# A decoder layer's FFNs: up products as seven products of half size in each dimension, tokens in quarters of 258

## The chip, the cores and the metric

The kernel runs on one core of a Trainium2 chip. The metric is the device time of one execution in microseconds. Five engines work side by side, each in the order of its own instructions, and wait for one another by semaphores: PE (TensorE, matrix products into PSUM), DVE (VectorE), ACT (ScalarE), POOL (GpSimd) and SP (SyncE, which issues most of the transfers).

## What is computed

One layer of a decoder for 1024 prompt tokens and 8 sample tokens, 1032 in all, with a width D of 1024: an FFN, a token mix (windowed attention and a gated branch), another FFN, and a last norm. All is float32. The part that the change touches is the FFN, which runs twice:

```python
def swiglu(h, w_up, w_down):
    a, b = jnp.split(h @ w_up, 2, axis=-1)
    return (jax.nn.silu(a) * b) @ w_down

def pre(i, t):
    return rms_norm(t, norm_g[i]) * (1 + mod[:, :, 3 * i + 1]) + mod[:, :, 3 * i]

x = x + 0.5 * mod[:, :, 2] * swiglu(pre(0, x), ffn1_up, ffn1_down)
```

`w_up` is 1024 x 5632 (two halves of D_FF = 2816, one for a and one for b), `w_down` 2816 x 1024. The shifts, scales and gates `mod` come from a product of the condition with `ada_w` (adaLN).

## The kernel before

**Layout.** Rows of weights lie on the 128 partitions, tokens along the free dimension. A large product gives 128 output rows for one chunk of tokens. The chunks `CH` are 384, 384 and 264 tokens wide. Both factors are split into a high and a low float32r part, and each product runs in three passes: high by high, high by low, low by high. `mm_chunk` (line 298) does this: it takes a PSUM buffer from the pool `ps_mm`, which has three, and for each k of the contraction issues the three matmuls of lines 306, 307 and 308.

**The FFN.** `ffn` (line 611) goes through 22 tiles of hidden rows in groups of `PARTS` (4, 4, 4, 4, 4, 2). For a tile and a chunk `up_a` makes the a half: ACT's tanh reads the PSUM buffer (line 626), DVE multiplies it with the same buffer (line 628). `up_b` makes the b half: DVE multiplies (line 641), ACT and DVE split the result into high and low part (642, 644). When a group is complete, its part of the down product is added to x in SBUF (`down_job`, `gated_add`, line 603, with lines 607 and 608 for the sample tokens). So up and down products alternate through the FFN.

**The weights** come as a stream of slabs of up to 1 MB, issued by SP (`fill_loads`, line 233); ACT copies the high part (272), DVE subtracts for the low part (273). Side work (adaLN products, norms, copies of caches) is cut into steps, and `tick()` between the matmuls advances it.

**The norm** (`norm`, line 539) reads x and writes high and low part of its result to tiles of their own: DVE multiplies (581), ACT adds the shift (583), DVE subtracts (571). The sums of squares are squared on ACT (486) and added on POOL (492).

**The start.** SP loads the adaLN weights of the first norm, the rows of x, the first slabs of `ffn1_up`; x is transposed by PE, and `mm_two` (line 318, matmuls 325 to 327) begins the first tile. x stays in SBUF through the first FFN and is copied to DRAM (`xs_d`) when each chunk of it is done.

## Time and profile before

| | us |
|---|---|
| median of 3 runs | 2422.71 (2422.45 to 2422.93) |
| span of the profiled execution | 2421.1 |
| PE busy | 2388.4 (99%) |
| PE weight loads busy | 2296.7 |
| DVE busy | 972.6 (40%) |
| ACT busy | 591.9 (24%) |
| POOL busy | 191.9 (8%) |

All later sums are made against the span; the median of the runs is 1.6 us longer, what lies around the program. Busy time of PE overlaps, since matmuls are pipelined: the distance of two starts tells the rate. PE's weight loads run beside its matmuls. An engine's idle time is listed with what released it, and idle time of an engine that isn't the bottleneck costs nothing.

### The profile page before, as it was taken

To read this page: it belongs to the slowest core of one execution; us is meant where nothing else is said; L and a number is where in the kernel's file an instruction comes from. 1 tells how busy PE (TensorE), PEld (TensorE's weight loads), DVE (VectorE), ACT (ScalarE), POOL (GpSimd) and SP (SyncE) were. 2 spreads that over 40 slices of the span, in tenths; PEclk is the share of its full clock that TensorE was granted. 3 is DMA by queue.
4 is the path that set the end of the run, shared out by engine and by line. 5 is a ranking of instruction groups with operands and counts; after the bars stand their busy time and mean duration, and the time that the engine had idled before them with its cause. 6 is when DMAs were issued, how large, how long until landed. Compare 5 with 4: busy or idle time off the path is not lost.

```text
span 2421.1 us, 36144 instructions
## 1 busy us (share of the span) xinstructions
PE 2388.4 (99%) x15567; PEld 2296.7 (95%) x15567; DVE 972.6 (40%) x1887; ACT 591.9 (24%) x1140; POOL 191.9 (8%) x285
## 2 busy tenths in 40 slices
...
GB/s 288 70 70 87 122 88 106 52 135 92 140 157 105 154 145 64 142 156 140 119 108 98 75 123 219 175 84 57 70 36 53 53 35 47 59 36 35 70 18 71
DMA packets 140649, 239.15 MB, mean 99 GB/s; under 512 B 6505, under 2 KB 98385, under 8 KB 139722
## 3 DMA queue, kind: packets, MB, share of 16 engines
...
q14 instruction: 37, 0.30, 0.0%
...
## 4 chain that ended last, share of the span: by engine, by line
PE 96%; DVE 1%; ACT 1%; DMA 1%; issue 0%; POOL 0%; DVEq 0%; SPq 0%; POOLq 0%; ACTq 0%
PE mm L306 30%; PE mm L307 29%; PE mm L308 29%; PE sc L398 1%; PE sc L986 1%; PE pv L1038 1%; DMA big<-in_ada_w_dram 1%; PE pt L1021 0%; PE mm L1021 0%; PE pt L421 0%; PE sc L1312 0%; DVE big L571 0%; PE ms L1237 0%; PE pt L1237 0%; DVE big L603 0%
## 5 line engine op out<-in xcount | busy, mean ns | idle before, releaser
L306 PE MATMUL mm<-big,hi 128*128 128x384 f32 (+1 forms) x4400 | 1420.0, 323 | 0.5 <-DVE t L1394 0.5
L308 PE MATMUL mm<-big,lo 128*128 128x384 f32 (+1 forms) x4400 | 1400.6, 318 | 0.0
L307 PE MATMUL mm<-big,hi 128*128 128x384 f32 (+1 forms) x4400 | 1400.0, 318 | 0.0
L306 PEld LDWEIGHTS mm<-big,hi 128*128 128x128 f32 x4400 | 827.0, 188 | 44.5 <-issue 26.1
L307 PEld LDWEIGHTS mm<-big,hi 128*128 128x128 f32 x4400 | 827.5, 188 | 0.2 <-DVE big L571 0.2
L308 PEld LDWEIGHTS mm<-big,lo 128*128 128x128 f32 x4400 | 826.2, 188 | 0.0
L272 ACT ACTIVATE hi<-raw 128x1024 fp32r<-128x1024 f32 (+1 forms) x186 | 194.1, 1043 | 448.3 <-PE mm L307 352.8
L273 DVE TENSOR_TENSOR lo<-raw,hi 128x1024 fp32r<-128x1024 f32 (+1 forms) x181 | 219.5, 1213 | 164.0 <-ACT hi L272 163.4
L603 DVE SCALAR_TENSOR_TENSOR big<-mm,MOD,big 128x384 f32<-128x384 f32 (+1 forms) x288 | 164.0, 571 | 235.9 <-PE mm L308 235.8
L628 DVE SCALAR_TENSOR_TENSOR t<-t,mm 128x384 f32<-128x384 f32 (+1 forms) x132 | 67.6, 512 | 287.7 <-ACT t L626 287.6
L641 DVE TENSOR_TENSOR t<-t,mm 128x384 f32<-128x384 f32 (+1 forms) x132 | 67.6, 512 | 276.4 <-PE mm L308 276.3
L642 ACT ACTIVATE big<-t 128x384 fp32r<-128x384 f32 (+1 forms) x132 | 64.9, 491 | 453.3 <-DVE t L641 453.3
L626 ACT ACTIVATE t<-mm 128x384 f32<-128x384 f32 (+1 forms) x132 | 60.4, 457 | 324.5 <-PE mm L308 324.5
L492 POOL TENSOR_TENSOR ph<-ph,t 128x384 f32<-128x384 f32 (+1 forms) x42 | 39.0, 930 | 797.4 <-ACT t L486 796.3
L644 DVE TENSOR_TENSOR big<-t,big 128x384 fp32r<-128x384 f32 (+1 forms) x128 | 66.2, 517 | 71.5 <-ACT big L642 71.5
L492 POOL TENSOR_TENSOR big<-big 128x384 f32<-128x384 f32 (+1 forms) x20 | 18.4, 921 | 721.8 <-ACT big L486 721.0
L1010 ACT ACTIVATE t<-t,s 128x128 f32<-128x128 f32 (+1 forms) x96 | 42.1, 439 | 80.3 <-DVE s L1005 72.8
L890 ACT ACTIVATE t<-mm 128x384 f32<-128x384 f32 (+1 forms) x48 | 21.9, 457 | 128.7 <-PE mm L308 92.8
L583 ACT ACTIVATE big<-t,MOD 128x384 fp32r<-128x384 f32 (+1 forms) x72 | 41.2, 579 | 47.8 <-DVE t L581 47.4
L571 DVE SCALAR_TENSOR_TENSOR big<-t,MOD,big 128x384 fp32r<-128x384 f32 (+1 forms) x72 | 46.6, 647 | 2.1 <-ACT big L583 2.1
L918 DVE COPY big<-mm 128x384 f32<-128x384 f32 x18 | 13.3, 741 | 59.7 <-PE mm L308 59.7
L306 PE MATMUL mm<-big 128*128 128x384 f32 (+1 forms) x96 | 33.0, 344 | 2.9 <-DVE big L603 2.2
...
## 6 DMA issues: line engine op xcount, KB each, us to landing
...
```

Source lines behind the costliest of these rows:

```text
L272: nc.scalar.activation(h3, v, AF.Copy)
L273: lo_eng[0].tensor_tensor(l3, v, h3.bitcast(FT), op=ALU.subtract)
L306: mm_f(ps[:, :n], wh, ah, start=(k == 0), stop=False)
L307: mm_f(ps[:, :n], wh, al, start=False, stop=False)
L308: mm_f(ps[:, :n], wl, ah, start=False, stop=(k == K - 1))
L492: nc.gpsimd.tensor_tensor(accs[c][0], accs[c][0], s, op=ALU.add)
L603: nc.vector.scalar_tensor_tensor(x[:, m, c0:e1], ps[:, :n], MOD[:, gate + m, 0:1], src[:, :n], op0=ALU.mult, op1=ALU.add)
L626: nc.scalar.activation(t[:, :w], pa[:, :w], AF.Tanh, scale=0.5)
L628: nc.vector.scalar_tensor_tensor(u[:, :w], t[:, :w], 1.0, pa[:, :w], op0=ALU.add, op1=ALU.mult)
L641: nc.vector.tensor_tensor(u[:, :w], u[:, :w], pb[:, :w], op=ALU.mult)
L642: nc.scalar.activation(g[:, s, c0:c1], u[:, :w], AF.Copy)
L644: eng.tensor_tensor(g[:, 4 + s, c0:c1], u[:, :w], g[:, s, c0:c1].bitcast(FT), op=ALU.subtract)
```

## The change

**Up products by Strassen's scheme.** The four blocks of a product of two by two blocks are a (two token quarters) and b (two token quarters): the contraction of 1024 is cut in two halves, the tokens of a pair in two quarters of 258 (256 of the prompt, 2 samples), and the output rows are the a and the b tile of one hidden tile. Instead of eight products of half the contraction there are seven, between sums and differences of the blocks. The sums over the tokens are made once in each FFN and pair of quarters (`pair_norm`, seven operands `H`), those of the weights for each hidden tile (`take`, on POOL). Products 0, 2, 4 and 6 are added up in the first of three accumulators of PSUM, product 1 goes to the second, 3 and 5 to the third (`ACC`); an accumulator has one bank for each of the two pairs. Results are read between the products (`finish`). One hidden tile for both pairs is a turn of 7 x 2 x 12 matmuls; the first two hidden tiles are done for pair 0 and then for pair 1, as four turns with one pair.

**Order.** All up products of an FFN come first, their gated results go to DRAM (`g_d`); the down products follow in `PARTS` (2, 4, 4, 4, 4, 4), with g loaded back and split, and x loaded back from `xs_d` or `x2_d`. All other large products run over four quarters of 258 tokens instead of three chunks.

**PSUM and SBUF.** The PSUM pools give way to one tile `PSB` whose eight banks are dealt out by stage. The norm works in place on x, and x is saved to DRAM ahead of it (`keep_x`).

The constants and the deal of the banks:

```diff
-PARTS = (4, 4, 4, 4, 4, 2)
-CH = ((0, 384), (384, 768), (768, 1032))
-ORD = (2, 0, 1)
+PARTS = (2, 4, 4, 4, 4, 4)
+QW = 258
+PW = 516
...
+    PSB = psp.tile([P, 8, 512], FT, name="PSB")
...
+    UPPER = dict(sc=(6,), pt=(7,), pv=(1,), ms=(3,))
+    LOWER = dict(two=(2, 4, 0), pt=(7,), pv=(6,), ms=(7,))
```

The large products outside of the up products:

```diff
-    def mm_chunk(w, j, K, act, c, k0=0):
...
+    def mm_chunk(w, j, K, act, c):
+
+        ps = bank("mm")[:, :QW]
...
-            if k % 2 == 1 and k < K - 1:
+            mm_f(ps, wh, ah, start=(k == 0), stop=False)
+            mm_f(ps, wh, al, start=False, stop=False)
+            mm_f(ps, wl, ah, start=False, stop=(k == K - 1))
+            if k in (2, 5) and k < K - 1:
```

The norm in place, the seven operands, and the copy of x:

```diff
+    def halves(t):
+
+        w = qb(FR, "h")
+        hi, lo = (four(w[:, z:z + 1032]) for z in (0, 1032))
+        nc.scalar.activation(hi, t, AF.Copy)
+        nc.vector.tensor_tensor(lo, t, hi.bitcast(FT), op=ALU.subtract)
+        return w
...
+    def pair_norm(i, p, rs, b0, blocks, stop=False, xs=None):
...
+            for k in range(4 * h, 4 * h + 4):
+                v = x[h][:, k % 4]
+                nc.vector.scalar_tensor_tensor(two(v), two(v), MOD[:, gp + k, 0:1], pb, op0=ALU.mult, op1=ALU.mult)
+                nc.scalar.activation(v, v, AF.Identity, bias=MOD[:, sh + k, 0:1])
...
+        H = OPS[p] = [None] * 7
+        f = nc.gpsimd.tensor_tensor
+        t3 = [tt().rearrange("p (k t) -> p k t", k=2) for _ in range(2)]
+        H[0] = halves(B[0][0])
+        for z in range(2):
+            f(t3[z], B[1][1][:, 2 * z:2 * z + 2], B[0][1][:, 2 * z:2 * z + 2], op=ALU.subtract)
+        f(B[0][1], B[0][1], B[0][0], op=ALU.subtract)
+        yield
+        H[1] = halves(B[1][0])
+        for z in range(2):
+            v = B[0][0][:, 2 * z:2 * z + 2]
+            f(v, v, t3[z], op=ALU.add)
+        yield
+        H[2] = halves(B[0][0])
+        yield
+        w = H[3] = qb(FR, "h")
+        for z in range(2):
+            hi, lo = (w[:, o_ + z * PW:o_ + z * PW + PW].rearrange("p (k t) -> p k t", k=2) for o_ in (0, 1032))
+            nc.scalar.activation(hi, t3[z], AF.Copy)
+            nc.vector.tensor_tensor(lo, t3[z], hi.bitcast(FT), op=ALU.subtract)
+        yield
+        nc.vector.tensor_tensor(B[1][0], B[1][0], B[0][0], op=ALU.subtract)
+        H[4] = halves(B[0][1])
+        yield
+        H[5] = halves(B[1][0])
+        yield
+        H[6] = halves(B[1][1])
...
+    def keep_x(p, dst):
+        for h in range(2):
+            nc.sync.dma_start(dst[:, 4 * h:4 * h + 4, p * PW:(p + 1) * PW], XT[p][h])
```

The up products, their weights, and what is read from PSUM when (`prepare` is the split of the weights before and `take` of these):

```diff
+    class Up:
+
+        ACC = (0, 1, 0, 2, 0, 2, 0)
+        AHEAD = 6
...
+            self.turns = [(0, (0,)), (1, (0,)), (0, (1,)), (1, (1,))] + [(n, (0, 1)) for n in range(2, NF)]
...
+        def take(self, s):
+            if s >= self.n:
+                return
+            n, j = divmod(s, 7)
+            a1, a2, b1, b2 = (self.raw[n][:, q * 512:(q + 1) * 512] for q in range(4))
+            w = hip.tile([P, 1024], FR, tag="hi", name=nm("hi")) if s % 2 else lop.tile([P, 1024], FR, tag="lo", name=nm("lo"))
+            f = nc.gpsimd.tensor_tensor
+            src = (a1, a2, a1, a1, b1, b2, a2)[j]
+            if j == 2:
+                f(b1, b1, b2, op=ALU.add)
+                f(a1, b1, a1, op=ALU.subtract)
+            elif j == 3:
+                f(a2, a2, a1, op=ALU.subtract)
+                f(a1, b2, a1, op=ALU.subtract)
+            self.wt[s] = w, src
...
+        def product(self, s):
+            n, j = divmod(s, 7)
+            w, _ = self.wt.pop(s)
+            go = dict(skip_group_check=True)
+            for p in self.turns[n][1]:
+                out = PSB[:, 2 * self.ACC[j] + p, :QW]
+                for kk in range(4):
+                    wh, wl = w[:, kk * 128:(kk + 1) * 128], w[:, 512 + kk * 128:512 + (kk + 1) * 128]
+                    h = OPS[p][j]
+                    ah, al = h[:, kk * QW:(kk + 1) * QW], h[:, 1032 + kk * QW:1032 + (kk + 1) * QW]
+                    mm_f(out, wh, ah, start=(kk == 0 and j in (0, 1, 3)), stop=False, **go)
+                    mm_f(out, wh, al, start=False, stop=False, **go)
+                    mm_f(out, wl, ah, start=False, stop=(kk == 3), **go)
+                    if kk % 2:
+                        tick()
...
+            def gate(v):
+                u = new()
+                nc.scalar.activation(u, v, AF.Tanh, scale=0.5)
+                nc.vector.scalar_tensor_tensor(u, u, 1.0, v, op0=ALU.add, op1=ALU.mult)
+                return u
+
+            if j == 0:
+                t["a"] = new()
+                nc.scalar.activation(t["a"], acc(0), AF.Copy)
+            elif j == 1:
+                nc.vector.tensor_tensor(t["a"], t["a"], acc(1), op=ALU.add)
+                t["u"] = gate(t.pop("a"))
+            elif j == 2:
+                t["b"] = new()
+                nc.scalar.activation(t["b"], acc(0), AF.Copy)
+            elif j == 3:
+                t["c"] = new()
+                nc.scalar.activation(t["c"], acc(2), AF.Copy)
+            elif j == 4:
+                nc.vector.tensor_tensor(t["c"], t["c"], acc(0), op=ALU.add)
+            elif j == 5:
+                nc.vector.tensor_tensor(t["b"], t["b"], acc(2), op=ALU.add)
+                u = t.pop("u")
+                nc.gpsimd.tensor_tensor(u, u, t.pop("b"), op=ALU.mult)
+                store(u, 0)
+            else:
+                u = gate(acc(0))
+                nc.gpsimd.tensor_tensor(u, u, t.pop("c"), op=ALU.mult)
+                store(u, 1)
+
+        def run(self, hook):
+            for s in range(self.n):
+                n, j = divmod(s, 7)
+                if j == 1:
+                    self.load(n + 2)
+                self.prepare(s + self.AHEAD)
+                if n < 4 and j == 0:
+                    require(self.turns[n][1][0])
+                self.product(s)
+                self.finish(s)
+                hook(n, j)
```

The down products (`split` makes high and low part of g on ACT and DVE, `job` is one down product with its gated addition):

```diff
+    class Down:
...
+        def load(self, i):
+            if i < len(PARTS):
+                self.raw[i] = self.rows([qb(name="g") for _ in range(self.count(i))], i)
+                for p in range(2):
+                    nc.gpsimd.dma_start(self.raw[i][p], self.src[:, self.FIRST[i]:self.FIRST[i] + PARTS[i],
+                                                                 p * PW:(p + 1) * PW])
...
+        def run(self, then, final):
+            dealing(**LOWER)
+            ahead = None
+            for i in range(len(PARTS)):
+                if ahead in hi_q:
+                    hi_q.remove(ahead)
+                    for _ in ahead:
+                        pass
+                if i == len(PARTS) - 1:
+                    run([self.job(i, m, p, qs, then) for p, qs in final for m in range(8)])
+                    return
+                ahead = self.split(i + 1, 6 if i == 0 else 0)
+                hi_q.append(ahead)
+                if i:
+                    self.load(i + 2)
+                run([self.job(i, m, p, (0, 1), lambda *_: None) for n in range(0, 8, 2) for p in range(2) for m in (n, n + 1)])
```

The order of the start:

```diff
+    for t in range(4):
         load_x(t)
-    fill_loads()
+    up1.load(0)
...
+    up1.load(1)
+    for t in range(4, 8):
         load_x(t)
+    nc.sync.dma_start(cst[:, C_M0:], a["consts"][:, C_M0:])
...
+    for t in range(1, 4):
+        turn_x(t)
+    keep_x(0, xs_d)
+    n0 = pair_norm(0, 0, first_rs(0), 4, True, True)
...
+        keep_x(1, xs_d)
+        yield from pair_norm(0, 1, first_rs(1), 6, True)
```

**Where instructions stand.** PE at the step from one tile of an up product to the next, in the middle of the first FFN, before; `mm` is a buffer of the pool, `hi` and `lo` are the weights; in brackets stand the semaphores that an instruction waits for (DMAHW and DMASW count transfers):

```order
L306 MATMUL mm_4410<-big_283,hi_4044 128x264
L307 MATMUL mm_4410<-big_367,hi_4044 128x264
L308 MATMUL mm_4410<-big_283,lo_4045 128x264
L306 MATMUL mm_4445<-big_283,hi_4225 128x384 [waits DVE_49,Activation_49]
L307 MATMUL mm_4445<-big_283,hi_4225 128x384
L308 MATMUL mm_4445<-big_283,lo_4226 128x384
```

The same after, at the step from one turn to the next; `PSB` is the PSUM tile with all banks, `h` an operand, and weights lie in tiles named `hi` or `lo`:

```order
L636 MATMUL PSB<-h_723,lo_4377 128x258
L637 MATMUL PSB<-h_723,lo_4377 128x258
L638 MATMUL PSB<-h_723,lo_4377 128x258
L636 MATMUL PSB<-h_372,hi_4409 128x258 [waits DVE_49]
L637 MATMUL PSB<-h_372,hi_4409 128x258
L638 MATMUL PSB<-h_372,hi_4409 128x258
```

Before, the next tile begins in another buffer (524 after 520) and waits for earlier readers of that; now the first matmul of the next turn waits for DVE on the banks that the matmul before it has just written.

DVE at the same place, before:

```order
L644 TENSOR_TENSOR big_4050<-t_4402,big_4050 128x264 [waits Activation_49]
L273 TENSOR_TENSOR lo_4439<-raw_4200,hi_4438 128x1024 [waits Activation_49]
L628 SCALAR_TENSOR_TENSOR t_4472<-t_4470,mm_4445 128x384 [waits Activation_49]
L641 TENSOR_TENSOR t_4472<-t_4472,mm_4474 128x384 [waits DVE_49,PE_49]
L644 TENSOR_TENSOR big_4050<-t_4472,big_4050 128x384 [waits Activation_49]
```

And after; `raw` are the weights of up products, `L657` the gate, `L673` and `L675` additions of accumulators:

```order
L673 TENSOR_TENSOR t_5145<-t_5145,PSB 128x516 [waits PE_49]
L620 TENSOR_TENSOR hi_5149<-raw_4836,hi_5149 128x512 [waits Activation_49]
L675 TENSOR_TENSOR t_5113<-t_5113,PSB 128x516 [waits PE_49]
L620 TENSOR_TENSOR lo_5179<-raw_4836,lo_5179 128x512 [waits DMAHW1_49,Activation_49]
L657 SCALAR_TENSOR_TENSOR t_5234<-t_5234,PSB 128x516 [waits DMASW0_49,Activation_49]
L620 TENSOR_TENSOR hi_5209<-raw_4836,hi_5209 128x512 [waits Activation_49]
```

The second of the gates' lines (L657) of a turn now stands between two weight splits, and it is the instruction for which PE's first matmul of the next turn waits.

SP at the end of the loads of the start, before:

```order
L359 DMA big_96<-in_x_prompt_dram 128x1024 [waits DMAHW6_49]
L359 DMA big_96<-in_x_prompt_dram 128x1024 [waits DMAHW7_49,PE_49,Activation_49]
L359 DMA big_96<-in_x_prompt_dram 128x1024 [waits DMAHW0_49]
L801 DMA cst<-in_consts_dram 128x776 [waits DMAHW1_49]
L233 DMA raw_275<-in_ffn_up_dram 128x8x128 [waits DMAHW2_49,Pool_49]
L233 DMA raw_281<-in_ffn_up_dram 128x8x128 [waits DMAHW3_49,Pool_49]
```

And after:

```order
L328 DMA xin_136<-in_x_prompt_dram 128x1024 [waits DMAHW0_49]
L328 DMA xin_139<-in_x_prompt_dram 128x1024 [waits DMAHW1_49]
L328 DMA xin_139<-in_x_prompt_dram 128x1024 [waits DMAHW2_49]
L844 DMA cst<-in_consts_dram 128x776 [waits DMAHW3_49]
L577 DMA xs_d<-x_185 128x4x516 [waits DMAHW4_49,DVE_49,Activation_49]
L577 DMA xs_d<-x_186 128x4x516 [waits DMAHW5_49,DVE_49]
L596 DMA raw_440<-in_ffn_up_dram 128x8x128 [waits DMAHW6_49,DVE_49,Pool_49]
```

The copy of x to DRAM (`xs_d`), which before was made at the end of the first FFN alone, now stands behind all loads of the start as well, and the next slab of weights behind it. DVE's first operation of the norm waits for the same counter (DMAHW4) as the first half of the copy uses, since it overwrites what is copied.

## Rows read from the trace of the kernel before

**Rows 1.** The page: busy us (share) xinstructions by engine; the chain by engine.

```profile
PE 2388.4 (99%) x15567; PEld 2296.7 (95%) x15567; DVE 972.6 (40%) x1887; ACT 591.9 (24%) x1140; POOL 191.9 (8%) x285
PE 96%; DVE 1%; ACT 1%; DMA 1%; issue 0%; POOL 0%; DVEq 0%; SPq 0%; POOLq 0%; ACTq 0%
```

**Rows 2.** Timeline of PE at a tile change: start us, us, engine, line, operation.

```profile
404.33 0.33 PE L306 MATMUL mm<-big,hi 128*128 128x384 f32 x1
...
405.89 0.28 PE L306 MATMUL mm<-big,hi 128*128 128x264 f32 x1
...
408.67 0.28 PE L308 MATMUL mm<-big,lo 128*128 128x264 f32 x1
```

**Rows 3.** Windows: stretch, busy time of each engine (instructions), clock, DMA share, GB/s.

```profile
2000.00:2300.00 300.00, 300.00 (x1920) 300.00 (x1920) 107.17 (x194) 51.23 (x80) 0.00 (x0) 1.00 0.15 50
```

**Rows 4.** Lines by form, PE, 0 to 110 us: xcount | busy us, mean ns.

```profile
L306 PE MATMUL mm<-big,hi 128*128 128x384 f32 x71 | 23.9, 337 | 0.0
...
L306 PE MATMUL mm<-big,hi 128*128 128x264 f32 x32 | 9.2, 286 | 0.0
...
L325 PE MATMUL mm<-big,hi 128*128 128x384 f32 x16 | 7.3, 458 | 3.6 <-ACT big L583 3.6
```

**Rows 5.** Timeline, all engines, from a tile's last matmul to its gate.

```profile
399.86 0.34 PE L308 MATMUL mm<-big,lo 128*128 128x384 f32 x1
...
400.30 0.49 ACT L626 ACTIVATE t<-mm 128x384 f32<-128x384 f32 x1 [3.76 <-PE mm L308]
400.82 0.56 DVE L628 SCALAR_TENSOR_TENSOR t<-t,mm 128x384 f32<-128x384 f32 x1 [4.27 <-ACT t L626]
```

**Rows 6.** Lines by form, whole span: tanh (L626) and gate (L628).

```profile
L628 DVE SCALAR_TENSOR_TENSOR t<-t,mm 128x384 f32<-128x384 f32 x88 | 48.8, 554 | 219.2 <-ACT t L626 219.2
...
L626 ACT ACTIVATE t<-mm 128x384 f32<-128x384 f32 x88 | 43.2, 491 | 243.1 <-PE mm L308 243.1
...
L628 DVE SCALAR_TENSOR_TENSOR t<-t,mm 128x264 f32<-128x264 f32 x44 | 18.9, 429 | 68.4 <-ACT t L626 68.4
...
L626 ACT ACTIVATE t<-mm 128x264 f32<-128x264 f32 x44 | 17.2, 390 | 81.3 <-PE mm L308 81.3
```

**Rows 7.** Timeline of the start: the first large matmul, SP's last load.

```profile
27.57 0.69 PE L325 MATMUL mm<-big,hi 128*128 128x384 f32 x1 [1.43 <-ACT big L583]
...
31.59 0.33 SPq L801 DMA_DIRECT2D cst<-in_consts_dram  x1
```

**Rows 8.** Windows at the end of the first loads.

```profile
45.00:46.00 1.00, 1.00 (x6) 1.00 (x6) 1.00 (x4) 0.62 (x1) 0.00 (x0) 0.69 0.83 198
46.00:47.00 1.00, 1.00 (x5) 1.00 (x4) 0.84 (x3) 0.91 (x2) 0.00 (x0) 0.50 0.10 29
```

**Rows 9.** Lines by form: an operation of 516 columns on DVE, of 384 on POOL.

```profile
L492 POOL TENSOR_TENSOR ph<-ph,t 128x384 f32<-128x384 f32 x28 | 28.5, 1017 | 60.8 <-ACT t L486 60.2
...
L1358 DVE TENSOR_TENSOR big<-big,big 128x516 fp32r<-128x516 f32 x12 | 8.3, 690 | 0.0
```

**Rows 10.** Timeline of DVE and POOL, one operation beside POOL and the same before.

```profile
833.38 0.47 DVE L571 SCALAR_TENSOR_TENSOR big<-t,MOD,big 128x256 fp32r<-128x256 f32 x1
...
835.14 2.16 POOL L492 TENSOR_TENSOR ph<-ph,t 128x384 f32<-128x384 f32 x2 [0.30 <-ACT t L486]
835.22 1.21 DVE L571 SCALAR_TENSOR_TENSOR big<-t,MOD,big 128x256 fp32r<-128x256 f32 x1
```

**Rows 11.** Lines by form: the gated addition of a down product.

```profile
L603 DVE SCALAR_TENSOR_TENSOR big<-mm,MOD,big 128x384 f32<-128x384 f32 x192 | 117.6, 615 | 173.0 <-PE mm L308 172.9
```

**Rows 12.** Timeline of PE: two pauses, idle before in brackets.

```profile
53.22 0.80 PE L553 MATMUL sc<-cst,mis 128*128 128x128 f32 x4 [1.22 <-POOL mis L470]
...
833.21 0.41 PE L306 MATMUL mm<-big 128*128 128x384 f32 x1 [2.17 <-DVE big L603]
```

**Rows 13.** Windows behind these two pauses.

```profile
54.00:55.00 1.00, 1.00 (x7) 1.00 (x7) 0.91 (x3) 0.43 (x1) 1.00 (x1) 1.00 0.58 185
834.00:835.00 1.00, 1.00 (x4) 0.99 (x4) 1.00 (x3) 0.61 (x3) 0.83 (x1) 0.50 0.91 263
```

1188 lines of the change are left out of this document (568 added, 620 removed).

## The prediction

> **What bounds the kernel now.** I read the page's busy line first: PE is busy for 99% of the span and no other engine for more than 40%; then the chain that ended last: PE holds 96% of it [rows 1]. So time is won or lost by PE's instruction stream, and only where PE stops. The timeline of one tile change gives the price of that stream: nine matmuls of 384 columns start in 405.89 − 404.33 = 1.56 us, 173.3 ns each; the 23 of 264 columns behind them start in 408.67 − 405.89 = 2.78 us, 120.9 ns each [rows 2]. A quiet stretch of 300 us agrees: 1920 matmuls, 156.25 ns each, where (2 × 173.3 + 120.9) / 3 is 155.8 [rows 3]. The durations of single matmuls overlap and say nothing of the rate. One weight position costs one triple, 384 + 384 + 264 columns, 467.5 ns. The program has 4608 positions (FFNs' up products 2 × 44 × 8) times three passes, 13,824 matmuls: 2112 triples are the up products, 2496 the rest.
>
> The rest of the span is a start in which PE mostly waits, the attention, and a tail. In the first 110 us PE issued 71 + 70 + 70 + 3 × 16 = 259 large matmuls of 384 columns and 96 of 264 [rows 4] (those rows show the first pass of each, the other two have 70, 70, 16, 16, 32 and 32): 44.9 + 11.6 = 56.5 us, so 53.5 us of the 110 did not stream.
>
> **The change part by part.** All sums are against the profiled span, 2421.1 us; the median of the runs is 1.6 above it.
>
> A. *Streaming.* A line through the two rates has 0.437 ns for a column, so 258 columns cost 118.3 ns, and four quarters 473.2. The up products go from 2112 triples, 987.4 us, to 44 × 7 × 2 × 12 = 7392 matmuls of 258, 874.5 us: −112.9. The other 2496 positions rise by 5.7 ns each: +14.2. A = −99. If 258 columns cost no less than 264, A is 7392 × 0.1209 + 2496 × 0.4836 − 2154.2 = −53.
>
> A rule that speaks against halving: in the Trainium skill, page "TensorE: Matmul & The Clock Gate", section "Back-to-back issue gap", a stream of weight loads and matmuls is spaced by both, about 81 ns at 128 columns and 131 at 512. On that line an estimate is 98 ns for 258 columns and 114 for 384, narrow matmuls would be dear, and the change would cost time by itself. The trace disagrees, 120.9 and 173.3 ns, a slope of 0.44 and not 0.10. The same section's formula for an isolated matmul, columns over 2.4 GHz plus 2.5 ns, gives 110 ns for 258 and by it A would be −105; I keep the measured rates.
>
> B. *A new wait at each turn's end.* Before, the first matmul of a tile goes to another PSUM buffer than the last one's. Now the last of the seven products of a turn leaves its result in banks 0 and 1, and the first product of the next turn starts there, so PE waits until ScalarE's tanh and VectorE's gate have read them, with no matmul between. That handoff is in the trace: the last matmul starts at 399.86 and takes 0.34, tanh starts at 400.30, the gate at 400.82 [rows 5]: 0.10 and 0.03 us from one to the next. At 516 columns, continued from 384 and 264, tanh takes 0.60 and the gate 0.69 [rows 6]. With 0.28 for the last matmul [rows 2] and 0.06, between the two handoffs, until PE starts: 0.28 + 0.10 + 0.60 + 0.03 + 0.69 + 0.06 − 0.12 (a slot that is paid anyway) = 1.65 us, 19 full turns in each FFN. 38 × 1.65 = 62.7; the second FFN's single-pair turns add about 3. B = +66. Range 55 (the two reads at 384 columns' price, 1.05 instead of 1.29) to 80 (each gate queued behind a part of a weight split of 0.69). The weight splits, additions and POOL's products inside a turn are covered: about 12 operations of VectorE at 0.69 are 8.3 us in a turn of 168 × 0.118 = 19.9.
>
> C. *The start.* Before, the first large matmul is at 27.57 [rows 7], while the loads still run: SP's last load of the start is issued at 31.59, and DMA falls from 198 to 29 GB/s between the 46th and 47th microsecond [rows 8]. Now the norm overwrites x in place, and so its first VectorE operation waits for the copy of x to DRAM, which SP issues behind all loads of the start, some 15 MB. I take the loads to end near 46 as before and the 1.06 MB of the copy to land near 50. Behind it, on VectorE in its order: four norm products (0.75 each, an estimate from 0.69 for 516 columns [rows 9]) and ScalarE's part, to 54; two groups of modulation, to 57; five weight splits, held by four POOL additions of 512 columns in a chain (1.35 each, by 1.02 for 384 [rows 9]), to 64; four more norm products, to 68; ScalarE's copy of 1032 columns, and the first matmul of an up product stands near 69. POOL's additions for the operands (1032 columns, 2.7 each) put the third operand near 77 and the seventh near 83. Pair 1's four blocks of x then pass ScalarE at some 3 us each, between the copies of the turn, so that turn 0 ends near 100 and turn 1 near 111; pair 1's own copy, norm and operands reach the first matmuls of turn 2 late, and the fourth single-pair turn ends near 135 (each of these an estimate by hand from the durations named). The four turns stream 336 × 0.1183 = 39.8 us, so some 95.5 us of 135 don't stream, 42 more than before. With 2 for a clock at 1.2 GHz after long stops and 3 for VectorE held up beside POOL (four times 0.74, the row below), C = +47. Range 25 (pair 1's work covered by the turns of pair 0) to 55.
>
> VectorE beside POOL: an operation that took 0.47 at 833.38 took 1.21 at 835.22, while POOL's additions ran from 835.14 on [rows 10].
>
> The Trainium skill, page "SBUF — State Buffer", section "SBUF: two separate sides", has a rule for it: a port pair that the two engines share is held by one instruction at a time, and the other blocks until it ends. By it each of VectorE's subtractions in the start that meets one of POOL's additions waits it out; with six such meetings of 1.35 an estimate of C is 52, the sum +42, the time 2465. The row agrees with the rule for one meeting.
>
> D. *The second FFN's start.* Pair 1's norm and seven operands are covered by the two turns of pair 0 alone, 19.9 us, where VectorE's share (8 × 0.75 + 7 × 1.4 + splits) and POOL's chain come to 25 to 35 in one queue: +12, range 3 to 18.
>
> E. *Down products.* They follow the up products as one block; the first part has K = 2: 16 jobs of 12 matmuls are 22.7 us of PE, against VectorE's gated additions (0.615 for 384 columns [rows 11]; I put 512 with the two small operations of the samples at 1.1) of 17.6 and the splits of the next part, 8 of 1032 columns at twice 0.69 [rows 9], 11: 6 too many, of which I put a third into the slack of the next part, +4 in each FFN, E = +8, range 2 to 14.
>
> F. *The end and the mix.* Quarters instead of chunks at the end: +3, range 0 to 6. The loads that are added (g back from DRAM, two more passes of x) lie under PE's stream: nothing; the queue moved 50 GB/s in the quiet stretch [rows 3].
>
> Sum: −99 + 66 + 47 + 12 + 8 + 3 = +37, a span of 2458, a time of about 2460.
>
> **Rivals.**
> R1, *the start is no longer: faster.* If the copy of x does not queue behind the loads, the norm starts near 27 as before; with C = 10 and D = 3 the sum is −99 + 66 + 10 + 3 + 8 + 3 = −9, a time of 2414. It decides from C + D below 17. For it: the copy's bytes are few. Against: its place, last on SP's queue, and DMA is loaded until 46 [rows 8].
> R2, *the pauses take the clock with them.* After the pause of 2.17 us that ends at 833.21 the granted clock was 0.50, the 1.2 GHz level, in three rows of one microsecond from 834 on; after one of 1.22 us that ends at 53.22 it stayed at 1.00 [rows 12, 13]. The new pause of 1.65 lies between. Three microseconds and their edges at half rate lose 1.5 to 1.7 us: 38 × 1.7 = +65, a time of 2525.
> R3, *narrow matmuls are not cheaper than 264 columns:* A = −53, a time of 2506. Against: one straight line fits both widths and the mean of 1920 matmuls [rows 2, 3].
> R4, *the pause is short* (a bank is released by the read of its half, or the queues run ahead): B near 25, a time of 2419, no change. Against: both reads span both banks.
>
> **How the numbers follow.** A measurement of this kernel can tell about 0.2%, 4.8 us, from no change. Forecast (2430 to 2490): 0.66; R1 0.10; R2 0.13; R3 0.05; R4 0.06. Range: from below R4 to between the forecast's upper bound and R2, 2415 to 2515, which leaves out R1's lower part and the upper half of R2. Faster: R1, 0.10. Same: R4 and the forecast's low edge, 0.08. Slower: 0.82.
>
> **What would show it.** Right: matmuls of 258 columns 118 ns apart; before the first product of nearly every full turn an idle time near 1.5 us on PE, released by VectorE's gate, as the largest entry of PE's waits; the first up product near 69, turn 2 near 124; granted clock 1.00 in the turns. Wrong: a first product before 45, idle times of under a microsecond at the turns' ends, a clock of 0.5 behind them, or a spacing above 121 ns.

## The result, and the profile after

The changed kernel takes 2574.3 us (median; 2573.1 to 2578.8), the kernel before 2422.6 on the same chip: 1.063 times as long, interval 1.061 to 1.064. So it is slower, as forecast, but by 152 us where 37 were expected, and above the range of 2415 to 2515.

The head of the page of the changed kernel: the span, the busy time of each engine with its share and its number of instructions, the chain that ended last, and the granted clock of PE and the busy share of POOL in 40 slices of 64 us, in tenths:

```profile
span 2571.0 us, 44780 instructions
...
PE 2360.5 (92%) x19191; PEld 2264.6 (88%) x19191; DVE 1162.2 (45%) x2154; ACT 777.0 (30%) x1499; POOL 678.6 (26%) x652
...
POOL 0454344444100110001100002234544444440003
PEclk7589999999999999999999999998799999999999
...
PE 26%; DVE 2%; ACT 1%; issue 0%; POOL 0%; DVEq 0%; ACTq 0%; POOLq 0%
```

Against [rows 1], PE is busy for 92% of the span instead of 99%: it has stops. No other engine is near its limit over the whole span (VectorE 45%), so what is late may be late by its place in an order, not by the amount of work. POOL, hardly used before (8%), works in both FFNs' up products, where it adds the weights' blocks. The clock line has its gaps in two places only, in the first three slices and in the 28th and 29th: the starts of the two FFNs. PE's waits of the changed kernel, by the line that waits and what it waited for (us in total, times, longest):

```profile
PE PSB L636 <- DVE t L657: 73.2, 44, 7.6
PE PSB L395 <- ACT t L389: 24.5, 2, 23.8
PE PSB L636 <- ACT t L668: 16.1, 4, 10.5
PE PSB L289 <- DVE s L1557: 15.1, 1, 15.1
PE PSB L636 <- ACT h L500: 13.3, 1, 13.3
PE PSB L853 <- ACT x L857: 10.1, 1, 10.1
```

The largest entry is the wait that the prediction named, before the first product of a turn (line 636), released by VectorE's gate (657). One such turn's end, from the timeline of the changed kernel (start, duration, engine, line, operation, idle time before it and its releaser):

```profile
422.36 0.28 PE L638 MATMUL PSB<-h,hi 128*128 128x258 f32 x1
...
422.68 0.60 ACT L656 ACTIVATE t<-PSB 128x516 f32<-128x516 f32 x1 [5.37 <-PE PSB L638]
...
423.31 0.69 DVE L657 SCALAR_TENSOR_TENSOR t<-t,PSB 128x516 f32<-128x516 f32 x1 [2.21 <-ACT t L656]
...
424.06 0.39 PE L636 MATMUL PSB<-h,lo 128*128 128x258 f32 x1 [1.42 <-DVE t L657]
```

The same handoff as in [rows 5], with 0.60 and 0.69 us for the two reads, exactly as continued from [rows 6], but now with no other matmul for PE to do.

To see where the 150 us of span went I cut both kernels at the ends of their stages and took from each stage the time that its large matmuls need at the distance that they have in uninterrupted runs: before, 174.1 ns at 384 columns and 121.4 at 264; after, 120.0 ns at 258. What is left over is time in which PE did not stream at that rate: it waited, did small work, or ran at the low clock.

| stage (span before; after) | not streaming before | after | difference |
|---|---|---|---|
| FFN 1 (0 to 844.3; 0 to 919.5) | 100.3 | 75.8 + 62.2 + 68.3 + 16.0 | +122.0 |
| mix (to 1656.4; to 1772.7) | 135.7 | 142.3 + 19.6 | +26.2 |
| FFN 2 (to 2409.7; to 2561.5) | 9.3 | 45.3 + 33.0 + 13.2 | +82.2 |
| tail | 11.4 | 9.5 | −1.9 |
| all streaming | 2164.4 | 2085.6 | −78.8 |

The four numbers of FFN 1 after are the time ahead of the first up product, the four single-pair turns, the full turns and the down products; in FFN 2 they are the single-pair turns, the full turns and the down products with the last norm; in the mix the second number is the output projection. The sum, −78.8 + 228.5, is the span's +149.9 but for rounding. By the letters of the prediction: **A** −79 instead of −99. **B** +65 instead of +66 (33.0 in FFN 2, and 68.3 less the 36.6 that stay in the run without that wait, below). **C**, the start, is 75.8 + 62.2 − 53.5 = +85 instead of +47. **D**, FFN 2's single-pair turns, +45 instead of +12. E and F together +10 instead of +11: in FFN 1 the 36.6 and 16.0 against 46.8 of before behind its 110th microsecond, +6, and in FFN 2 13.2 − 9.3, +4. The **mix**, which the prediction put at nothing, +26.

The start, from the timelines of SP, POOL, ACT, DVE and PE of the changed kernel, in order of time:

```profile
40.12 0.93 SPq L577 DMA_DIRECT2D xs_d<-x  x2
...
52.36 2.74 DVE L525 SCALAR_TENSOR_TENSOR x<-x,MOD,PSB 128x516 f32<-128x516 f32 x4 [22.20 <-DMA xs_d<-x]
...
56.39 1.12 PE L395 MATMUL PSB<-cst,t 128*128 128x128 f32 x4 [23.76 <-ACT t L389]
...
75.06 3.51 POOL L544 TENSOR_TENSOR t<-x,x 128x516 f32<-128x516 f32 x2 [6.19 <-DVE x L528]
...
75.78 0.58 PE L636 MATMUL PSB<-h,lo 128*128 128x258 f32 x1 [13.33 <-ACT h L500]
...
83.98 1.06 ACT L500 ACTIVATE h<-x 128x1032 fp32r<-128x1032 f32 x1 [7.29 <-POOL x L550]
...
92.36 0.57 ACT L857 ACTIVATE x<-PSB 128x512 f32<-128x512 f32 x1
...
92.99 1.97 PE L853 MATMUL PSB<-cst,xin 128*128 128x128 f32 x8 [10.15 <-ACT x L857]
```

The norm waits for the copy of x, until 52.36 where 50 was forecast, and PE stands still for 23.8 us up to 56.39; the first up product stands at 75.78 (forecast 69). Then it falls behind at each step: the third operand needs three POOL sums in a row, PE's transposes of the second half of x (line 853) stand in PE's order between up products and wait for ScalarE's copies (857), and these stand in ScalarE's order behind the high parts of the operands (500), which wait for POOL. Turn 1 begins at 124.6 and turn 2 at 148.7 (forecast for the ends of turns 0 and 1: 100 and 111, and 124 for turn 2), and the four single-pair turns end at 178.3 (135). Three windows of the changed kernel (start:end, length, busy time and instructions of PE, PEld, DVE, ACT, POOL, then granted clock, DMA share, GB/s): the four single-pair turns of FFN 1, those of FFN 2, and 10 us in FFN 1's:

```profile
75.80:178.30 102.50, 67.55 (x400) 62.23 (x401) 64.77 (x95) 46.48 (x90) 48.96 (x42) 0.72 0.35 111
```

```profile
1772.70:1858.40 85.70, 55.47 (x363) 52.86 (x362) 54.54 (x77) 35.35 (x65) 46.58 (x39) 0.80 0.24 71
```

```profile
120.00:130.00 10.00, 5.38 (x24) 5.23 (x24) 7.31 (x7) 3.42 (x5) 8.04 (x6) 0.50 0.04 13
```

The four turns need 40.3 us of streaming and take 102.5 and 85.7. The granted clock falls to 0.50, the 1.2 GHz level, behind the long stops; matmuls of 258 columns are then 0.215 us apart. Of the 62.2 and 45.3 us lost, about 15 and 10 are the wider spacing of matmuls at that rate, and 35 and 30 are idle time (the window less PE's busy time); the rest, 12 and 5, was not taken apart (small matmuls and the edges of the stops).

The output projection, from the timelines of ACT, DVE and PE:

```profile
1739.29 1.06 ACT L500 ACTIVATE h<-x 128x1032 fp32r<-128x1032 f32 x1 [8.31 <-POOL x L550]
...
1740.38 1.23 DVE L501 TENSOR_TENSOR h<-x,h 128x1032 fp32r<-128x1032 f32 x1 [7.20 <-ACT h L500]
1741.53 1.29 DVE L558 TENSOR_TENSOR h<-t,h 128x516 fp32r<-128x516 f32 x2
1742.75 1.23 DVE L560 TENSOR_TENSOR x<-x,x 128x1032 f32<-128x1032 f32 x1
1743.89 3.59 DVE L501 TENSOR_TENSOR h<-x,h 128x1032 fp32r<-128x1032 f32 x3
1747.39 0.75 DVE L1553 SCALAR_TENSOR_TENSOR x<-PSB,MOD,t 128x512 f32<-128x512 f32 x1
1748.06 0.15 DVE L1557 TENSOR_TENSOR s<-PSB,MOD 128x4 f32<-128x4 f32 x1
```

```profile
1748.36 0.55 PE L289 MATMUL PSB<-m,hi 128*128 128x258 f32 x1 [15.13 <-DVE s L1557]
```

PE waits 15.1 us in one stop for the addition that reads the bank (1553 and 1557). That addition is short, 0.9 us; it stands in VectorE's order behind the operand steps of FFN 2's first pair (501, 558, 560), and VectorE itself waited 7.2 us there for ScalarE, and ScalarE 8.3 us for POOL's sums (550).

### The profile page after: what moved, and what is told of

It reads as the page before. It is cut to its first block, busy times and chain, and to the rows that moved or that the text cites. A ratio compares the mean times of both kernels' runs of the same rounds, so it can differ in the third digit from the quotient of the medians.

```text
span 2571.0 us, 44780 instructions
## 1 busy us (share of the span) xinstructions
PE 2360.5 (92%) x19191; PEld 2264.6 (88%) x19191; DVE 1162.2 (45%) x2154; ACT 777.0 (30%) x1499; POOL 678.6 (26%) x652
## 5 line engine op out<-in xcount | busy, mean ns | idle before, releaser
L636 PE MATMUL PSB<-h,hi 128*128 128x258 f32 x1232 | 360.0, 292 | 68.8 <-DVE t L657 45.6
L289 PE MATMUL PSB<-g,hi 128*128 128x258 f32 x1408 | 402.6, 286 | 8.7 <-DVE s L780 8.5
L636 PE MATMUL PSB<-h,lo 128*128 128x258 f32 x1232 | 359.0, 291 | 52.0 <-DVE t L657 27.7
L291 PE MATMUL PSB<-g,lo 128*128 128x258 f32 x1408 | 399.6, 284 | 0.0
L290 PE MATMUL PSB<-g,hi 128*128 128x258 f32 x1408 | 399.0, 283 | 0.0
L273 PE MATMUL PSB<-h,hi 128*128 128x258 f32 x1344 | 395.1, 294 | 2.3 <-ACT h L500 1.3
L274 PE MATMUL PSB<-h,hi 128*128 128x258 f32 x1344 | 381.2, 284 | 1.8 <-DVE h L501 1.8
L275 PE MATMUL PSB<-h,lo 128*128 128x258 f32 x1344 | 380.8, 283 | 0.0
L637 PE MATMUL PSB<-h,lo 128*128 128x258 f32 x1232 | 353.0, 286 | 1.1 <-DVE h L501 1.1
L637 PE MATMUL PSB<-h,hi 128*128 128x258 f32 x1232 | 353.7, 287 | 0.0
L638 PE MATMUL PSB<-h,hi 128*128 128x258 f32 x1232 | 353.2, 287 | 0.0
L638 PE MATMUL PSB<-h,lo 128*128 128x258 f32 x1232 | 351.9, 286 | 0.0
L636 PEld LDWEIGHTS PSB<-h,hi 128*128 128x128 f32 x1232 | 238.5, 194 | 87.5 <-DVE t L657 51.3
L636 PEld LDWEIGHTS PSB<-h,lo 128*128 128x128 f32 x1232 | 238.2, 193 | 70.1 <-DVE t L657 31.8
L289 PEld LDWEIGHTS PSB<-g,hi 128*128 128x128 f32 x1408 | 267.3, 190 | 11.3 <-DVE s L780 9.8
L273 PEld LDWEIGHTS PSB<-h,hi 128*128 128x128 f32 x1344 | 256.0, 190 | 23.5 <-issue 15.1
L290 PEld LDWEIGHTS PSB<-g,hi 128*128 128x128 f32 x1408 | 268.1, 190 | 0.0
L291 PEld LDWEIGHTS PSB<-g,lo 128*128 128x128 f32 x1408 | 266.9, 190 | 0.0
L274 PEld LDWEIGHTS PSB<-h,hi 128*128 128x128 f32 x1344 | 256.1, 191 | 2.2 <-DVE h L501 2.2
L275 PEld LDWEIGHTS PSB<-h,lo 128*128 128x128 f32 x1344 | 254.9, 190 | 0.0
L637 PEld LDWEIGHTS PSB<-h,lo 128*128 128x128 f32 x1232 | 238.5, 194 | 1.4 <-DVE h L501 1.4
L637 PEld LDWEIGHTS PSB<-h,hi 128*128 128x128 f32 x1232 | 239.3, 194 | 0.0
```

What stands on the lines that cost most here:

```text
L273: mm_f(ps, wh, ah, start=(k == 0), stop=False)
L274: mm_f(ps, wh, al, start=False, stop=False)
L275: mm_f(ps, wl, ah, start=False, stop=(k == K - 1))
L289: mm_f(ps[:, q, :], wh, h, start=(k == 0), stop=False)
L290: mm_f(ps[:, q, :], wh, l, start=False, stop=False)
L291: mm_f(ps[:, q, :], wl, h, start=False, stop=(k == K - 1))
```

## The experiments

**Theory** after this reading: the time is the sum of separate mechanisms, each in its own place: matmuls of 258 columns cost no less than those of 264; the turn's end costs 1.7 us, 38 times; the copy of x holds up the start because it is issued late; the work for the operands (POOL's sums, splits, norms) holds up PE wherever its steps stand in one order with something that PE waits for. **Rivals:** the copy is late because it lands late or is held whatever the queue; POOL's speed, not the order, sets the starts; the single-pair turns are too short for their own weights, whatever the second pair does.

### The matmul's price at nine widths

Kernel before, with 96 matmuls of each width, each with its weight load, behind the end:

```
+    for n in (384, 256, 258, 264, 300, 344, 384, 448, 512):
+        q = bank(ps_mm, "mm")
+        for i in range(96):
+            mm_f(q[:, :n], pw[:, i % 8 * 128:i % 8 * 128 + 128], pa[:, i % 4 * 128:i % 4 * 128 + n],
+                 start=(i == 0), stop=(i == 95))
```

> The kernel before, with a probe behind its end that adds no result: 96 matmuls each of 384, 256, 258, 264, 300, 344, 384, 448 and 512 columns, with a weight load for each. Theory: every matmul costs its columns at the 2.4 GHz level plus a fixed 11 to 14 ns, as the mean spacings of the two traces say (384: 174.1, 264: 121.4, 258: 120.0 ns), so 258 costs about 120, 300 about 138, 344 about 157, 512 about 227, and four quarters of 258 are dearer than the chunks 384, 384, 264 by about 10 ns per weight position and pass. Rival 1, the forecast's straight line of 0.437 ns a column: 258 at 118.3, 512 at 229. Rival 2, a floor by the weight loads: 256, 258 and 264 all at the same time, near 120, and 300 on a line from there to 384 (137).

Groups of instructions by shape in the added stretch (times, busy time in us, mean ns of one, idle):

```profile
L1535 PE MATMUL mm<-lo,hi 128*128 128x512 f32 x96 | 22.0, 389 | 0.0
...
L1535 PE MATMUL mm<-lo,hi 128*128 128x344 f32 x96 | 15.3, 319 | 0.0
L1535 PE MATMUL mm<-lo,hi 128*128 128x300 f32 x96 | 13.3, 298 | 0.0
L1535 PE MATMUL mm<-lo,hi 128*128 128x258 f32 x96 | 11.8, 283 | 0.0
L1535 PE MATMUL mm<-lo,hi 128*128 128x264 f32 x96 | 11.7, 281 | 0.0
L1535 PE MATMUL mm<-lo,hi 128*128 128x256 f32 x96 | 11.7, 283 | 0.0
```

The distance of two starts is busy time less one mean, divided by 95; measured over the second half of each run of 96 it is 120.0 ns at 256 columns, 120.8 at 258, 120.0 at 264, 136.6 at 300, 157.8 at 344, 173.4 at 384, 206.7 at 448 and 226.7 at 512. So 256, 258 and 264 columns cost the same within 0.8 ns, as the second rival has it, and the line through 264 and 384 columns does not go on to 258: it gives 118.3. That is what A lacks. The theory's fixed 11 to 14 ns above the columns at 2.4 GHz fails at 264 columns (10.0) and at 448 (20.0). That the weight loads set the floor is not shown: no run changes them.

### Two accumulators changed over in every other turn

The last product of a turn then leaves its result in banks that the next turn does not begin with (the reads follow, and the deal of the banks for the down products, `two`, becomes (4, 0, 2)):

```
-        ACC = (0, 1, 0, 2, 0, 2, 0)
+        ACC = ((0, 1, 0, 2, 0, 2, 0), (1, 0, 1, 2, 1, 2, 1))
...
-                out = PSB[:, 2 * self.ACC[j] + p, :QW]
+                out = PSB[:, 2 * self.ACC[n % 2][j] + p, :QW]
```

> The changed kernel, with the first and second accumulator swapped in every other turn, so that the first product of a turn goes to banks that were released two products before; nothing else. Theory: the stop of 1.42 us at the end of each full turn (38 of them, 1.69 us from turn to turn) goes, the time falls by 55 to 65 us from 2574 to about 2514, and full turns of the second FFN take 20.2 us instead of 21.8. Rival: VectorE and ScalarE are late in every turn anyway, the wait moves to the second product, and less than 15 us is won.

Measured: 2504.6 us, 1.033 times before (1.032 to 1.035), 70 us less than the changed kernel, a little more than expected. A full turn of FFN 2 takes 20.13 us instead of 21.81, and what FFN 2's full turns do not stream falls from 33.0 us to under 1, in FFN 1 from 68.3 to 36.6. PE's waits for the gate in this kernel (its lines are one further):

```profile
PE PSB L636 <- DVE t L658: 13.7, 4, 6.3
```

Four of 44 waits are left, those of the single-pair turns. So the pauses are B, 1.7 us each with what belongs to them; 20.13 / 168 is 119.8 ns a matmul, the same as the probe.

### The copy of x from other queues

Two kernels: the copy's issue on ScalarE's queue, and on GpSimd's.

```
-    keep_x(0, xs_d)
+    keep_x(0, xs_d, nc.scalar)      # the other kernel: nc.gpsimd
...
-        keep_x(1, xs_d)
+        keep_x(1, xs_d, nc.scalar)
```

> The changed kernel, with the two copies of x at the start issued from ScalarE's queue instead of SP's; nothing else. Theory: the norm of the first pair waits for a copy that stands behind the loads, so its first operation moves from 52.4 to about 35 us, the first up product from 75.8 to about 59, and the time falls by 12 to 20 us from 2574. Rival: the transfers share the same 16 engines, so the copy lands near 50 wherever it is issued, and nothing is won; or the weights and the groups of modulation become the bound and less than 6 us is won.

> The changed kernel, with the two copies of x at the start issued from GpSimd's queue; nothing else. From ScalarE's queue the copy was issued only at 38.7 us (SP's: 40.1), behind the loads' transfer counters, and the time did not move. Theory: GpSimd's queue has counters of its own, the copy is issued near 29 and lands by 38, the norm starts 12 to 16 us earlier, the first up product near 61, and the time falls by 10 to 18 us from 2574. Rival: the loads keep the 16 engines full until 50 us, the copy lands near 48 whatever issues it, and less than 5 us is won.

From ScalarE's queue: 2573.2 us, 1.062 (1.060 to 1.064), no change. From GpSimd's: 2559.7, 1.057 (1.055 to 1.058), 15 us less. Timelines of the first and of the second kernel:

```profile
38.73 2.18 ACTq L577 DMA_DIRECT2D xs_d<-x  x2
...
50.43 2.74 DVE L525 SCALAR_TENSOR_TENSOR x<-x,MOD,PSB 128x516 f32<-128x516 f32 x4 [20.02 <-DMA xs_d<-x]
```

```profile
27.70 1.70 POOL L577 DMA_DIRECT2D xs_d<-x  x2
...
37.91 2.74 DVE L525 SCALAR_TENSOR_TENSOR x<-x,MOD,PSB 128x516 f32<-128x516 f32 x4 [6.96 <-DMA xs_d<-x]
```

The copy lands some 10 to 12 us behind its issue in all three kernels; what differs is the issue, at 40.1, 38.7 and 27.7. So the copy is not slow behind the loads; its issue is held on SP's and ScalarE's queues and not on GpSimd's. The semaphore events in the first kernel's trace show what holds it on ScalarE's: right before the issue the queue waits, until 38.67, for semaphore 104. In it the copy will count its landing, and a load of adaLN weights that SP issued at 24.62 counted its own there; the last part of that load landed at 38.65. On GpSimd's queue the copy counts in semaphores 111 and 112, which no load of the start uses. SP comes to the copy only at 40.1, behind its last loads of x. The first up product moves to 61.3, 14.5 earlier, and the whole gain reaches the end: nothing covered it.

### The sums of the operands: on VectorE, further apart, or not at all

Three kernels. On VectorE instead of POOL (five instructions for each pair of quarters; the sixth sum is on VectorE already):

```
-        f = nc.gpsimd.tensor_tensor
+        f = nc.vector.tensor_tensor
```

> The changed kernel, with the sums for the operands of the up products (six additions for each pair of quarters, in both FFNs) on VectorE instead of GpSimd; nothing else. Theory: the stops of PE at the two FFNs' starts and in the out projection (15.1 us before 1748, 10.2 before 93, 7.6 before 1802, 10.5 before 1820) are the chain of these sums, of 2 to 3.5 us each on GpSimd, with everything queued behind it on ScalarE and VectorE; with 0.7 to 1.2 us each on VectorE the stops shrink and the time falls by 15 to 35 us from 2574. Rival: VectorE's own queue is what is full there, 7 us more work for each pair makes the stops longer, and the time rises by 5 to 20 us.

The operand steps of FFN 2's first pair four steps of side work apart instead of one:

```
+        gap = 4 if i == 2 and p == 0 else 1
...
-        yield
+        yield from rest(gap)            # at each of the six steps
```

> The changed kernel, with the seven operand steps of the second FFN's first pair of quarters four steps of the side queue apart instead of one, inside the out projection; nothing else. Theory: PE's stop of 15.1 us before 1748 is a backlog: the steps are queued on VectorE and ScalarE faster than they run (one every 0.8 us, 1.2 to 2.5 us each), and the out projection's additions stand behind them; spread out, the stop shrinks below 6 us and the time falls by 8 to 15 us from 2574. Rival: the operands' chain itself is what is waited for; they are only ready later, the stop moves to the first up product of the second FFN, and the time stays within 4 us.

Without the sums over the tokens, VectorE's one too (the operands are then the blocks as they are, and the splits stay):

```
-        f = nc.gpsimd.tensor_tensor
+        f = lambda *_, **__: None
...
-        nc.vector.tensor_tensor(B[1][0], B[1][0], B[0][0], op=ALU.subtract)
```

> The changed kernel without the sums and differences of token blocks (in both FFNs; the seven operands are plain blocks, so the up products are not the reference's); the splits of the operands into high and low part, the norm and everything else stay. Theory: the sums are a part of the stops at the FFNs' starts, but the splits (seven of 1032 columns on ScalarE and VectorE each) and the norm, queued in order ahead of the turn's reads, are the larger one: the time falls by 15 to 30 us from 2574 and at least 60 us of the 108 that do not stream in the first four turns and the out projection's stop remain. Rival: the sums on GpSimd are the chain, and without them the stops all but vanish: the time falls by 60 us or more.

| kernel | us | times before | less than the changed kernel |
|---|---|---|---|
| sums on VectorE | 2564.2 | 1.059 (1.057 to 1.060) | 10 |
| steps further apart | 2564.7 | 1.058 (1.057 to 1.060) | 10 |
| no sums | 2539.1 | 1.048 (1.046 to 1.050) | 35 |

Spacing the steps, with no work taken away, brings the stop in the output projection down from 15.1 to 5.0 (two waits), as PE's waits of that kernel show, and what the projection does not stream falls from 19.6 to 10.2: there it is the order.

```profile
PE PSB L289 <- DVE s L1558: 5.0, 2, 4.1
```

On VectorE the sums do not hold up more than on POOL, though VectorE is the busier engine, but they win less than the 15 to 35 us expected: the single-pair turns of FFN 1 lose 56.9 instead of 62.2, and the stop 11.7 instead of 15.1. Even without any sum the three stages still lose 47.0, 35.1 and 11.5, 93.6 of 127.1 us. So the sums over the tokens are a quarter of the delay; the rival that their speed on POOL sets the starts falls. The sums of the weights (`take`) stayed on POOL in every run, and for them the rival was not tested; the last experiment's trace comes back to them.

### All of it together, and the second half of x earlier

The accumulators, the copies on GpSimd's queue, the sums on VectorE, the spacing, and the first six weight splits ahead of the first norm:

```
...
+    keep_x(0, xs_d, nc.gpsimd)
+    for s in range(up1.AHEAD):
+        up1.prepare(s)
     n0 = pair_norm(0, 0, first_rs(0), 4, True, True)
...
```

> The changed kernel with the swapped accumulators, the copies of x on GpSimd's queue, the splits of the first six weights ahead of the first norm, the sums on VectorE and the second FFN's first operands spread out, all together. Theory, from the parts: 70 for the accumulators, 10 to 18 for the copy, 6 to 9 for the splits of the weights (they would run while VectorE waits for the copy), 10 for the sums, 8 for the spreading: 2455 to 2475. Rival: the starts are bound by one chain, of which each part only shifts a piece, and the time is above 2485. Both theories leave it slower than the kernel before, 2423.

2464.3 us, 1.017 (1.016 to 1.019): 110 us less, where four of the five changes gave 70 + 15 + 10 + 10 alone; the fifth, the weight splits ahead of the norm, was not run alone, and the first up product stands 7 us earlier than with the copy alone. So the parts add up within a few microseconds, as separate places would. It still takes 41 us longer than the kernel before. The first up product stands at 54.1, but the single-pair turns still lose 57.3 and 42.7 us. To find what, the second half of x was loaded, transposed and copied at the start too (first kernel below; the second is the same with another bank for the transposes):

```
...
+    new_x(1)
+    dealing(pv=(7,))                # the second kernel only
+    for t in range(4, 8):
+        turn_x(t)
+    keep_x(1, xs_d, nc.gpsimd)
...
```

> The kernel of e10_all, with the second half of x loaded before the last groups of modulation weights, and transposed, copied and summed up at the start behind the first half norm, and not inside the first turn; nothing else. Theory: in the first turn PE stops 8.1 us for ScalarE's reads of these transposes and some 8 us of its queue are theirs, while ScalarE and VectorE are idle before 40 us; the time falls by 10 to 20 us from 2464. Rival: the start is bound by the norm, splits and sums of the two pairs in one order, the work only changes its place, and the time stays within 5 us.

> The kernel of e11_x, but with the transposes of the second half of x through another bank of PSUM (in e11_x and e12_eight they overwrote the first pair's 1/rms ahead of the second half of its norm, so values there are not the reference's). Theory: the instructions and their times are the same, 2455 to 2464. Rival: the bank is shared with the groups of modulation, and the time rises above 2468.

2459.5, 1.015 (1.013 to 1.017), and 2458.8, 1.015 (1.013 to 1.017). FFN 1's turns then lose 46.0 us instead of 57.3, but the first product moves from 54.1 to 59.6: 5 us are won, as the rival had it, and half of the work has only moved ahead. The second is the fastest version with all of the work; it takes 36 us longer than the kernel before.

### What the single-pair turns lose

More of them (eight, four for each pair), so that pair 0's turns cover more of pair 1's preparation; and the version "all together" with no norm and operands of pair 1, which then computes with pair 0's:

```
-            self.turns = [(0, (0,)), (1, (0,)), (0, (1,)), (1, (1,))] + [(n, (0, 1)) for n in range(2, NF)]
+            self.turns = [(n, (p,)) for p in range(2) for n in range(4)] + [(n, (0, 1)) for n in range(4, NF)]
```

> The kernel of e11_x, with four hidden tiles for the first pair of quarters and then for the second, instead of two, in both FFNs (eight turns with one pair; each costs its weights' sums and splits again); nothing else. Theory: the second pair's norm and operands, some 25 us of VectorE's queue, now lie beside 40 us of PE's work and not 20, so the stops in the turns before the second pair's first product (7.7, 6.1 and others, about 25 us in the second FFN) shrink by half: 10 to 25 us less over both FFNs. Rival: VectorE's own weight splits fill the new turns (7 of 10 us), the backlog stays as long, and the time is within 6 us or longer.

```
+        if p == 1 and blocks:
+            OPS[1] = OPS[0]
+            return
```

> The kernel of e10_all without the norm and the operands of the second pair of quarters ahead of the up products, in both FFNs (the second pair's products take the first pair's operands, so the results for it are not the reference's); copies of x, products and everything else stay. Theory: what stops PE in the turns with one pair is this work, queued in order on VectorE and ScalarE among the turns' reads and splits: in the second FFN the four turns fall from 83 us to 42 to 48, in the first from 98 to 60 to 75, and the time from 2464 to 2390 to 2410, below the kernel before. Rival: the turns with one pair are short of VectorE by themselves (their splits and sums for 10 us of PE), and the four turns stay above 65 us in the second FFN.

Eight turns: 2480.0, 1.024 (1.022 to 1.025), 20 us *more* than with four: the 10 to 25 us less of the theory did not come. Windows of FFN 2's single-pair turns, with all together (four turns), and with eight:

```profile
1701.00:1784.00 83.00, 57.20 (x362) 54.22 (x361) 55.25 (x82) 35.53 (x66) 38.48 (x35) 0.77 0.25 73
```

```profile
1704.00:1838.00 134.00, 100.37 (x694) 95.90 (x693) 89.22 (x130) 57.87 (x113) 72.96 (x68) 0.85 0.45 149
```

Four turns lose 83.0 − 40.3 = 42.7 us, eight (to 1838.6) 134.6 − 80.6 = 54. A turn of one pair has half of PE's work, 10.1 us, but the whole of the weight sums and splits; VectorE is busy for two thirds of both stretches. Each further turn costs some 2.8 us of its own.

Turn by turn the traces show why nothing was won: turns 0 and 1 take 23.8 and 34.8 us in both kernels, and each turn behind them 11.6 to 14.5. The side queue gives out a step for every six matmuls, so pair 1's norm and operands still run in turns 0 and 1 (on VectorE from 1720.5 to 1758.8), and the added turns cover nothing. The same steps spread over four turns, as in the output projection, were not tried; whether cover is lacking stays open.

Without pair 1's norm and operands: 2415.1, 0.997 (0.996 to 0.998), 49 us less. FFN 2's four turns take 56.4 instead of 83.0 and lose 16.1 instead of 42.7; those of FFN 1 lose 32.6 instead of 57.3. So 25 us in FFN 1 and 27 in FFN 2 are the second pair's norm and operands. In FFN 2 the other 16 us are the turns themselves, 8 in the first and 2.4 to 2.9 in each of the others; of the 33 left in FFN 1 one stop before the transposes of the second half of x is 8.6. PE's largest wait in this kernel is released by a combination behind the gate (678), not by an operand:

```profile
PE PSB L640 <- DVE t L678: 11.2, 7, 3.5
```

Four of the seven are in FFN 2's four turns, one in each, 0.9 to 1.8 us long. The first of them, from the timelines of ACT, DVE and PE:

```profile
1691.70 0.63 ACT L623 ACTIVATE hi<-raw 128x512 fp32r<-128x512 f32 x1 [1.02 <-POOL raw L614]
...
1692.37 1.23 DVE L624 TENSOR_TENSOR hi<-raw,hi 128x512 fp32r<-128x512 f32 x1 [1.84 <-ACT hi L623]
1693.52 0.41 DVE L678 TENSOR_TENSOR t<-t,PSB 128x258 f32<-128x258 f32 x1
...
1693.98 0.39 PE L640 MATMUL PSB<-h,lo 128*128 128x258 f32 x1 [0.88 <-DVE t L678]
```

The combination stands in VectorE's order behind a weight split (624), which waits for ScalarE's copy (623), and that for one of POOL's sums of the weights (614); the other three show the same chain. So the weights' sums on POOL take part here, which no run moved.

Neither forecast came: the four turns' 56.4 us lie between the theory's 48 and the rival's 65, and the time is above the theory's 2410. Both are part of it, some two thirds to one. Even without this work the kernel only takes as long as the one before.

## Why the prediction was right or wrong

**What bounds the kernel: right.** PE's stream and its stops decide; every microsecond taken from a stop came out at the end, alone (70, 15, 10, 10) and together (110).

**A: the step that failed is the line.** "A line through the two rates has 0.437 ns for a column, so 258 columns cost 118.3 ns": 120.0 were measured, in the changed kernel, and 120.8 in the probe. Over 17,376 matmuls that is 30 us too few. Against it the stream of before was put 10 short, 2154.2 for the 2164.4 that its distances give over the whole program: −79 instead of −99. R3's statement was right, narrow matmuls are not cheaper than 264 columns; its A of −53 came from 120.9 ns for both, where 120.0 makes 15 us of difference, and from the same 10. The page "TensorE: Matmul & The Clock Gate" of the Trainium skill, section "Back-to-back issue gap", fares no better on the probe: an estimate on the line between its figures for a stream, 81 ns at 128 columns and 131 at 512, is 98 for 258 columns, and its formula for a matmul alone gives 110; the chip gave 120.8, and 226.7 at 512. (The slope of that line is 0.13, not the 0.10 of the prediction, and the 4608 "positions" there are triples, one for each position and pass; neither touches the sum.)

**B: right, size and mechanism.** 1.65 us for each end of a turn was the sum (its terms give 1.64), 21.81 − 20.13 = 1.68 is measured; the two reads took the 0.60 and 0.69 that were continued from smaller shapes. R4 (a short pause) did not happen. R2 (the clock falls with each pause) did not either: a stretch of FFN 2's full turns with one pause in every 21.8 us keeps the clock at 1.00.

```profile
1900.00:2200.00 300.00, 280.18 (x2310) 277.24 (x2309) 110.10 (x165) 93.64 (x166) 139.02 (x111) 1.00 0.49 172
```

**C: right in its first wait; the step that failed is the one chain behind it.** The norm behind the copy of x (52.4 for "near 50"), and so the fall of R1, came as forecast. Of the 38 us too few, 7 lie ahead of the first product, and some 31 in the four turns. There the prediction added durations by hand along one chain (its 95.5 should read 95.2, which changes nothing). What it left out is that four orders are coupled: the second half of x passes PE and ScalarE *between* the products and the operands' splits, so a late POOL sum holds ScalarE, ScalarE's copy holds PE's transposes, and these hold the products behind them. The runs give sizes that overlap: 15 us less in these turns without the sums, 11 less with the transposes moved ahead, 25 less without pair 1's norm and operands. And it put "2 for a clock at 1.2 GHz", where some 15 us were lost to it, since PE stopped again and again.

In these turns VectorE runs beside POOL. The subtraction of line 501 takes 1.23 alone, at 1740.38, and 1.51 in the mean of its 32 records over the whole span:

```profile
L501 DVE TENSOR_TENSOR h<-x,h 128x1032 fp32r<-128x1032 f32 x32 | 47.6, 1513 | 25.5 <-ACT h L500 25.5
```

The prediction weighed the rule of the shared port (the Trainium skill, "SBUF — State Buffer", "SBUF: two separate sides") with an estimate of 52 for C. The trace agrees, record by record: of the single subtractions those that begin while POOL is idle take 1.22 to 1.23, and the nine that begin well inside one of POOL's sums end 1.09 behind the end of that sum (at 77.36, for one, where the sum ends at 78.58 and the subtraction at 79.67). In the four turns of FFN 1 all of VectorE's operations take 11 us longer than the shortest of their form, 4 of them beside the sums over the tokens and 5 beside those of the weights, where C had 3. How much of this reached PE no run separates.

**D: the step that failed is the cover.** Pair 1's norm and operands were to be "covered by the two turns of pair 0 alone, 19.9 us, where VectorE's share (8 × 0.75 + 7 × 1.4 + splits) and POOL's chain come to 25 to 35 in one queue: +12". The prediction took the two turns of pair 0 as free to hide work and counted what is left over. But the steps of pair 1 stand in one order with the reads that free PE's banks, and cost 27 us instead of 12; and a turn of one pair does not hide its own weight work, which was put at nothing: the run without pair 1's work still loses 16 us. With the 3 that went with the edits made together, these make the 45.

**The missing term: pair 0's operands of FFN 2.** The prediction has no line for them: the norms of the kernel before lay under PE's stream, and I carried that over. The operands' steps are 1.2 to 3.6 us long, and they stand in VectorE's order ahead of the additions that free PE's banks. One stop of 15.1 us came from it, 10 of which went by spacing alone; for the rest of the mix's +26 no cause is shown: 6.6 us lie in the attention and the gated branch, and some 4 in the output projection behind its long stop.

**E and F: right in the sum** (+10 for +11), **in part by luck**. In E's place, the first part of the down products, the stops before gated additions are there but shorter than forecast: five of 0.3 to 0.5 us in FFN 1 (660.99 to 669.27), four in FFN 2. The longest stop of FFN 1's down products, 5.2 us before 912.92, is at their end and of the kind above: the addition that PE waits for stands in VectorE's order behind 4.7 us of splits of the mix's norm (501, from 907.49). The kernel before has 2.17 us at that place [rows 12].

Put together, in the span: 2458 + 20 (A) + 38 (C) + 33 (D) + 26 (mix), less 4 for B, E, F and the tail, is 2571.
